# Squared-ReLU MLPs: relu without the norm factor on ScalarE, the factor squared at the addition to the residual

## The chip, the core and the metric

The kernel runs on one core of one Trainium2 chip. The metric is the device time of one execution in microseconds (us). Times of a kernel are given as the median of several runs. The engines are TensorE (PE, with its weight loads PEld), VectorE (DVE), ScalarE (ACT), GpSimd (POOL) and SyncE (SP, which only issues transfers here). Each works through its own queue in order; an instruction that has to wait holds up everything behind it on its engine.

## The reference

A two-layer model on 256 tokens of width 2048, all in float32: `h = h + attention(rms_norm(h))`, then `h = h + mlp(rms_norm(h))`, with stick-breaking attention in the first layer and native sparse attention in the second. Only the MLPs are touched here:

```
def rms_norm(x, g):
    xf = x.astype(jnp.float32)
    y = xf * lax.rsqrt(jnp.mean(xf * xf, axis=-1, keepdims=True) + NORM_EPS)
    return (y * g.astype(jnp.float32)).astype(x.dtype)

def sqrelu_mlp(h, w1, w2):
    return jnp.square(jax.nn.relu(h @ w1)) @ w2

# in reference(), for each of two layers, D_FF = 8192
h = h + sqrelu_mlp(rms_norm(h, mlp_norm_g[layer]), mlp_w1[layer], mlp_w2[layer])
```

The factor `rsqrt(...)` is one positive number r for each token. Since relu(r x) = r relu(x) for a positive r, and the square of it is r squared times relu(x) squared, r may enter before the relu or, squared, after the second product.

## The kernel before

**Products.** Every float32 product is made of three TensorE products of parts: a value is split into a rounded upper part `hi` and a rest `lo`, and hi*hi, hi*lo and lo*hi are summed in PSUM. The weights come from DRAM in blocks of 256 rows by 512 columns (512 KB) through SP's queue into a ring of five buffers `raw` and, in the MLPs, a sixth (`raw6`). ScalarE rounds a block to `hi` (L142), VectorE subtracts it to get `lo` (L144). A block is free for the next load when both have read it. `hi` and `lo` have four buffers each. Activations are kept split as well: `xs` holds the normed input of a layer without r (transposed, with the gains), `yhi` and `ylo` the activations behind the relu.

**MLP.** `mlp` treats d_ff in four quarters `fg`. Each quarter has two phases:

- `group1` makes the quarter's 2048 columns of `h @ w1` in four blocks `fb` of 512, transposed: the PSUM tiles have the d_ff index on the partitions and the tokens along the row. A block is 8 chunks (`chunk_T`, L206, 24 products of 256 columns). Behind it come the relu and the factor (L444), the square (L449, `sq`), the split into `yhi` (L450) and `ylo` (L451), and sums of it for the Strassen scheme (L456 to L460, `sums` to `ss`).
- `group2` multiplies with the quarter's rows of `w2`: blocks `nb` of 512 output columns, each of 8 chunks (`chunk_N`, L173, 12 products of 512 columns), added to the residual `h` by `add_h` (L383).

One or two of the four output blocks of a quarter are made by a one-level Strassen scheme instead (`in_S`, `chunk_S`, L269, 21 products of 256 columns with 7 sums in place of 8): block 2 in the shadow of `group2`, and block 3 in the shadow of the next quarter's `group1`. VectorE makes the sums of weights for it (`ts`, L245, L248, L249), ScalarE and VectorE split three quarters of the raw block into `shi` (L247) and `slo` (L250, one buffer each) and `ts` into `hi` and `lo`. Eight chunks make a block; then `add_S` adds the seven PSUM halves to `h` (L293 to L301). The very last block of the second MLP goes to `add_out`, which adds and writes the output.

**The factor.** `make_rstd` gives r with the tokens on the partitions. `group1` needs it along the row, so `rows` transposes it twice by `bcast_rows` (L376) and ScalarE copies it to `row` (L422), a tile of 256 float32 in each partition.

**Order.** The loops are unrolled. Outside the first stretch of the kernel a scheduler sets the order of each engine's queue from the order in which the code stands, the dependencies and its own costs. `spawn` and `pump` set small pieces of work between the products of a chunk.

Of the kernel before, what the change touches and what calls it, by code (L numbers as in the profile page):

```python
# [8 lines left out]
F32 = mybir.dt.float32  # L9
F32R = mybir.dt.float32r  # L10
AF = mybir.ActivationFunctionType
OP = mybir.AluOpType
# [3 lines left out]
P = 128  # L16
T = 256
NT = T // P
# [23 lines left out]
def hybrid_kernel(  # L42
# [6 lines left out]
    nc = tc.nc  # L49
# [11 lines left out]
    h = cpool.tile([P, NT, D], F32, name="h")  # L61
# [47 lines left out]
    def spawn(gen, rate, wait=0.0, first=False):  # L109
        beside.insert(0 if first else len(beside), [gen, rate, -wait])  # L110
# [54 lines left out]
    def bank(pool, tag):  # L165
        return pool.tile([P, NB], F32, tag=tag, name=tag)
# [117 lines left out]
        half = lambda j, i: bs[j][:, i * W:(i + 1) * W]  # L284
        return bs, [half(0, 0), half(1, 0), half(1, 1), half(2, 0), half(2, 1), half(3, 1), half(3, 0)]

    def add_S(nb, bs, ps, pool):

        W = NB // 2
        uv = pool.tile([P, 4, W], F32, tag="pre", name="uv", bufs=1)  # L290
        u, v = uv[:, :2, :], uv[:, 2:, :]
        hb = [h[:, t, nb * NB:(nb + 1) * NB] for t in range(NT)]
        nc.scalar.activation(u[:, 0, :], ps[0], AF.Copy)  # L293
        nc.vector.tensor_tensor(v[:, 0, :], ps[5], u[:, 0, :], op=OP.add)
        nc.vector.tensor_tensor(u[:, 1, :], ps[4], v[:, 0, :], op=OP.add)
        nc.vector.tensor_tensor(v[:, 1, :], ps[6], v[:, 0, :], op=OP.add)
        nc.vector.tensor_tensor(hb[0], bs[1], hb[0], op=OP.add)
        nc.vector.tensor_tensor(hb[1], bs[2], hb[1], op=OP.add)
        nc.vector.tensor_tensor(hb[0], hb[0], u.rearrange("p a n -> p (a n)"), op=OP.add)
        hv = hb[1].rearrange("p (a n) -> p a n", a=2)  # L300
        nc.vector.tensor_tensor(hv, hv, v[:, 1, :].unsqueeze(1).to_broadcast([P, 2, W]), op=OP.add)  # L301

    def proj_N(src, n0, pool=acc, tag="acc", turn=False):
        ps = [bank(pool, tag) for _ in range(NT)]
# [59 lines left out]
    def make_rstd(layer):  # L364
        s = small.tile([P, NT], F32, tag="ms", name="ms")
        nc.vector.tensor_reduce(s, ssq_t[layer], axis=AX.X, op=OP.add)
        nc.vector.tensor_scalar(s, s, 1.0 / D, EPS, op0=OP.mult, op1=OP.add)
        r = small.tile([P, NT], F32, tag="rstd", name="rstd")
        nc.gpsimd.tensor_tensor(r, s, neghalf[:, :NT], op=OP.pow)
        return r  # L370

    def bcast_rows(rstd):

        ps = bank(att, "att")
        for t in range(NT):
            nc.tensor.transpose(ps[:, t * P:(t + 1) * P], rstd[:, t:t + 1].to_broadcast([P, P]), ident)  # L376
        return ps

    def add_h(nb, ps, scale=None):
        for t in range(NT):  # L380
            hb = h[:, t, nb * NB:(nb + 1) * NB]
            if scale is None:
                nc.vector.tensor_tensor(hb, ps[t], hb, op=OP.add)  # L383
            else:
                nc.vector.scalar_tensor_tensor(hb, ps[t], scale[:, t:t + 1], hb, op0=OP.mult, op1=OP.add)

    def add_out(nb, ps, ov):

        for t in range(NT):
            for i in range(2):  # L390
                w = NB // 2
                c = slice(nb * NB + i * w, nb * NB + (i + 1) * w)
                nc.vector.tensor_tensor(h[:, t, c], ps[t][:, i * w:(i + 1) * w], h[:, t, c], op=OP.add)
                (nc.sync, nc.scalar)[i].dma_start(ov[:, t, c], h[:, t, c])

    def out_proj(src, layer, g0):
# [17 lines left out]
    def mlp(l, layer, junk, done, last=None):  # L414
        w1, w2 = mlp_w1[l], mlp_w2[l]
        ss = far(junk, KD * 4 * P, "ss").rearrange("p (a k i n) -> p a k i n", a=2, k=KD // 2, i=4)
        row = junk.tile([P, T], F32, name="row", bufs=1)

        def rows():
            yield  # L420
            pb = bcast_rows(make_rstd(layer))
            nc.scalar.activation(row, pb[:, :T], AF.Copy)  # L422

        def in_S(fg, nb):

            for i in range(NK):
                if i == 0:
                    bs, s = banks_S(att, "att")
                chunk_S(s, w2, fg * KD + i * KC, nb * NB, i == 0, i == NK - 1, yhi, ylo, ss[:, 0], ss[:, 1],
                        koff=fg * KD)  # L430
                if i == NK - 1:
                    add_S(nb, bs, s, junk)
                yield

        def group1(fg, beside_w1):

            step = lambda: next(beside_w1)
            for fb in range(D // NB):
                ps = [bank(acc, "acc") for _ in range(NB // P // 2)]
                proj_T(ps, w1, fg * D + fb * NB, then={2: step, 5: step} if beside_w1 else {})  # L440
                k, n = fb * (NB // P), NB // P
                a = junk.tile([P, n, T], F32, tag="pre", name="pre", bufs=1)
                for j in range(0, n, 2):
                    nc.vector.scalar_tensor_tensor(  # L444
                        a[:, j:j + 2, :], ps[j // 2].rearrange("p (m t) -> p m t", m=2), 0.0,
                        row.unsqueeze(1).to_broadcast([P, 2, T]), op0=OP.max, op1=OP.mult,
                    )
                s = junk.tile([P, n, T], F32, tag="sq", name="sq", bufs=1)
                nc.scalar.activation(s, a, AF.Square)  # L449
                nc.scalar.activation(yhi[:, k:k + n, :], s, AF.Copy)  # L450
                nc.vector.tensor_tensor(ylo[:, k:k + n, :], s, yhi[:, k:k + n, :].bitcast(F32), op=OP.subtract)  # L451

                sv = s.rearrange("p (j kk) t -> p j kk t", kk=2)
                a1, a2 = [[sv[:, :, kk, t * P:(t + 1) * P] for kk in (1, 0)] for t in range(NT)]
                q = junk.tile([P, 2, 4, P], F32, tag="sums", name="sums", bufs=1)
                nc.vector.scalar_tensor_tensor(q[:, :, 0, :], a2[0], -1.0, a2[1], op0=OP.mult, op1=OP.subtract)  # L456
                nc.vector.tensor_tensor(q[:, :, 2, :], a1[0], a2[0], op=OP.subtract)
                nc.vector.tensor_tensor(q[:, :, 1, :], a2[1], q[:, :, 2, :], op=OP.subtract)
                nc.vector.tensor_tensor(q[:, :, 3, :], a1[1], q[:, :, 1, :], op=OP.subtract)
                split_evac(ss[:, 0, k // 2:k // 2 + 2], ss[:, 1, k // 2:k // 2 + 2], q)  # L460

        def group2(fg, end):

            blocks = (0, 1, 3) if end else (0, 1)
            side, si = in_S(fg, 2), 0
            for j in range(len(blocks) * NK):
                nb, i = blocks[j // NK], j % NK
                if i == 0:
                    ps = [bank(acc, "acc") for _ in range(NT)]
                out = last is not None and end and nb == 3  # L470
                aside = si < NK and j >= 4 + (1.75 if end else 1.4) * si
                chunk_N(ps, w2, fg * KD + i * KC, nb * NB, i == 0, i == NK - (2 if out else 1), yhi, ylo,
                        koff=fg * KD, by_token=out and i == NK - 1,
                        turn=aside or (not end and j == len(blocks) * NK - 1))
                if i == NK - 1:
                    if out:
                        add_out(nb, ps, last)
                        return
                    add_h(nb, ps)
                    if end and nb == 3:  # L480
                        done(nb, (att, "att"))
                if aside:
                    next(side)
                    si += 1
                    if si == NK and end:
                        for n in range(3):
                            done(n, (att, "att"))

        spawn(rows(), 1)
        NK = KD // KC  # L490
        for fg in range(DFF // D):
            group1(fg, in_S(fg - 1, 3) if fg else None)
            group2(fg, fg == DFF // D - 1)


    with tc.tile_pool(name="sbp", bufs=2) as sp:
# [11 lines left out]
        with tc.manual_schedule(engines={mybir.EngineType.PE, mybir.EngineType.DVE, mybir.EngineType.Activation,  # L508
# [47 lines left out]
            for i in range(NX):  # L556
# [4 lines left out]
                first, last = i == 0, i + 1 == NX  # L561
# [11 lines left out]
        rows = sp.tile([P, 2, T], F32, name="rows", bufs=1)  # L573
        factor = []
# [90 lines left out]
        for hg in range(NH // HG):  # L665
            qT = sp.tile([P, HG, T], F32, name="qT")
            kT = far(sp, HG * T, "kT", F32, 2).rearrange("p (j t) -> p j t", j=HG)
            v = far(sp, NT * NB, "v", F32, 2).rearrange("p (t n) -> p t n", t=NT)
# [36 lines left out]
    with tc.tile_pool(name="nsa", bufs=2) as ap, ExitStack() as last:  # L705
# [283 lines left out]
        for i in range(2):  # L989
            cT = cp.tile([P, G, T], F32, tag="cT", name="cT", bufs=1)  # L990
            for b in range(2):
                ps = proj_Th(w_in, C0 + i * NB + b * T)
                if rstd is None:
                    rstd = make_rstd("nsa")
                    pb = bcast_rows(rstd)
# [58 lines left out]
        for g in range(G):  # L1054
            ps = [bank(acc, "acc") for _ in range(NT)]
# [9 lines left out]
            v = ap.tile([P, 2, NT, 2, P], F32R, tag="v", name="v")  # L1065
# [6 lines left out]
            ps = proj_N(w_in, g * NB)  # L1072
# [11 lines left out]
    with tc.tile_pool(name="m1p", bufs=2) as mp:  # L1084
        wsum = sixth = mp
        ov = out[0].rearrange("(t p) d -> p t d", p=P)
# [35 lines left out]
```

## Time and profile before

| | |
|---|---|
| median of 3 runs | 2154.17 us (2151.66 to 2154.63) |
| profiled execution, its own time | 2150.99 us |
| its span, first to last instruction | 2149.3 us |
| TensorE busy | 2138.9 us |
| VectorE busy | 1594.8 us |
| ScalarE busy | 1189.7 us |
| granted TensorE clock | 1.000 |
| first MLP, about | 392 to 1075 us of the span |
| second MLP, about | 1460 us to the end |

How to read the lines that follow. A group's line has the line of code, engine, operation, `output<-inputs`, the shapes, and then "busy us, mean ns of one | idle time of the engine before them, and what ended it". A line of time has start, duration, engine, line and operation, with the idle time before it in brackets. A stretch's line has the stretch, its length, the busy time of PE, PEld, DVE, ACT and POOL with the number of instructions, the granted TensorE clock, the busy share of the DMA engines and the rate in GB/s. Matmuls overlap, so how long one takes in a stream is read from start to start.

### The profile page before, as it was taken

Reading aid. Unit: us, or ns where it says so; the run is one execution under the profiler, and the core shown is the slowest. Engines: PE = TensorE matmul, PEld = TensorE weight load, DVE = VectorE, ACT = ScalarE, POOL = GpSimd, SP = SyncE. Lnnn points to the kernel's source line nnn. Section 1 sums busy time; section 2 is a strip of 40 time slices with the busy share of each in tenths; the row PEclk is TensorE's granted clock in tenths of the full one; section 3 lists DMA queues with packets and bytes.
Section 4 is the critical chain, followed back from the end, with each engine's and each line's share of the span. In section 5 each row is a group of like instructions: output and inputs, shape, how many; then the busy total and the mean of one; then the engine's idle time right before and its main releaser. Section 6 shows DMA issues by size and latency. Waiting matters only on the chain.

```text
span 2149.3 us, 37266 instructions
## 1 busy us (share of the span) xinstructions
PE 2138.9 (100%) x14898; PEld 1974.0 (92%) x14898; DVE 1594.8 (74%) x2193; ACT 1189.7 (55%) x1591; POOL 43.3 (2%) x75
## 2 busy tenths in 40 slices
PE   9999999999999999999999999999999999999999
PEld 9999988998998999999898888889989989989998
DVE  5556556668879878779776887755788798787796
ACT  6555665555555555455655666655555555554463
POOL 0000000000000000000000011000000000000000
PEclk9999999999999999999999999999999999999999
DMA  7655556665665656665667554456656556566654
GB/s 238 211 170 177 159 183 187 185 199 180 203 201 189 210 188 203 216 195 188 200 187 220 162 147 139 146 177 187 191 184 210 191 189 209 184 199 211 197 194 159
DMA packets 260790, 406.35 MB, mean 189 GB/s; under 512 B 13188, under 2 KB 91912, under 8 KB 260616
## 3 DMA queue, kind: packets, MB, share of 16 engines
q1 hardware_dynamic: 259800, 403.52, 59.9%
q8 instruction: 116, 1.90, 0.3%
q10 hardware_dynamic: 816, 0.46, 0.1%
q14 instruction: 58, 0.48, 0.1%
HBM read 401.83 MB, written 2.10 MB: 188 GB/s over the span
## 4 chain that ended last, share of the span: by engine, by line
PE 95%; DVE 3%; DMA 1%; issue 1%; ACT 0%; POOL 0%; DVEq 0%; SPq 0%; ACTq 0%; POOLq 0%
PE acc L206 42%; PE acc L173 35%; PE att L269 12%; PE att L173 1%; DVE lo L144 1%; DMA raw<-in_mlp_w_dram 1%; PE att L327 1%; PE att L944 1%; DVE slo L250 0%; DMA raw<-in_nsa_w_in_dram 0%; PE att L655 0%; PE att L607 0%; PE att L882 0%; PE att L938 0%; PE att L884 0%
## 5 line engine op out<-in xcount | busy, mean ns | idle before, releaser
L142 ACT ACTIVATE hi<-raw 128x1024 fp32r<-128x1024 f32 x639 | 673.1, 1058 | 511.3 <-PE acc L206 231.9
L144 DVE TENSOR_TENSOR lo<-raw,hi 128x1024 fp32r<-128x1024 f32 x639 | 774.1, 1221 | 214.6 <-ACT hi L142 199.7
L206 PE MATMUL acc<-xs,hi 128*128 128x256 f32 x5360 | 665.4, 277 | 0.0
L206 PEld LDWEIGHTS acc<-xs,hi 128*128 128x128 f32 x5360 | 634.6, 188 | 0.9
L206 PE MATMUL acc<-xs,lo 128*128 128x256 f32 x2680 | 359.2, 276 | 0.0
L206 PEld LDWEIGHTS acc<-xs,lo 128*128 128x128 f32 x2680 | 329.2, 188 | 0.0
L173 PE MATMUL acc<-hi,yhi 128*128 128x512 f32 x828 | 324.4, 392 | 0.0
L173 PE MATMUL acc<-hi,ylo 128*128 128x512 f32 x828 | 323.0, 390 | 0.0
L173 PE MATMUL acc<-lo,yhi 128*128 128x512 f32 x828 | 224.1, 391 | 0.0
L245 DVE TENSOR_TENSOR ts<-raw 128x512 f32<-128x512 f32 x112 | 76.8, 690 | 184.2 <-DMA raw<-in_mlp_w_dram 184.0
L142 ACT ACTIVATE hi<-ts 128x1024 fp32r<-128x1024 f32 x112 | 118.6, 1059 | 125.0 <-PE acc L173 47.3
L173 PEld LDWEIGHTS acc<-lo,yhi 128*128 128x128 f32 x828 | 154.6, 188 | 31.6
L173 PEld LDWEIGHTS acc<-hi,ylo 128*128 128x128 f32 x828 | 155.5, 188 | 29.6 <-DVE ylo L314 0.2
L173 PEld LDWEIGHTS acc<-hi,yhi 128*128 128x128 f32 x828 | 155.5, 188 | 29.6 <-ACT yhi L313 0.2
L173 PE MATMUL acc<-hi,xs 128*128 128x512 f32 x704 | 177.2, 392 | 0.0
L173 PEld LDWEIGHTS acc<-hi,xs 128*128 128x128 f32 x704 | 130.2, 188 | 26.2
L144 DVE TENSOR_TENSOR lo<-ts,hi 128x1024 fp32r<-128x1024 f32 x112 | 136.5, 1219 | 2.2 <-ACT hi L142 2.1
L247 ACT ACTIVATE shi<-raw 128x768 fp32r<-128x768 f32 x112 | 94.4, 843 | 77.6 <-DMA raw<-in_mlp_w_dram 28.3
L250 DVE TENSOR_TENSOR slo<-raw,shi 128x768 fp32r<-128x768 f32 x112 | 106.7, 952 | 2.6 <-PE att L269 2.5
L449 ACT ACTIVATE sq<-pre 128x1024 f32<-128x1024 f32 x32 | 34.0, 1063 | 128.5 <-DVE pre L444 128.5
L173 PE MATMUL acc<-lo,xs 128*128 128x512 f32 x352 | 97.0, 396 | 0.0
L269 PE MATMUL att<-hi,ss 128*128 128x256 f32 x672 | 94.4, 276 | 0.0
(249 smaller groups left out, 2170.6 us busy)
## 6 DMA issues: line engine op xcount, KB each, us to landing
raw<-in_mlp_w_dram SPq DMA_DIRECT2D x512, 512.0 KB, 4.4
raw<-in_sb_w_qkv_dram SPq DMA_DIRECT2D x95, 512.0 KB, 3.8
raw<-in_nsa_w_in_dram SPq DMA_DIRECT2D x50, 512.0 KB, 3.8
raw<-in_sb_w_out_dram SPq DMA_DIRECT2D x32, 512.0 KB, 3.9
raw<-in_nsa_w_in_dram SPq DMA_DIRECT2D x64, 256.0 KB, 3.9
raw<-in_nsa_w_out_dram SPq DMA_DIRECT2D x32, 512.0 KB, 3.6
w1t<-in_nsa_cmp_w_dram SPq DMA_DIRECT2D x8, 512.0 KB, 4.1
h<-in_x_dram SPq DMA_DIRECT2D x8, 256.0 KB, 4.5
```

Source lines behind the costliest of these rows:

```text
L142: nc.scalar.activation(hi, raw, AF.Copy)
L144: nc.vector.tensor_tensor(lo, raw, hi.bitcast(F32), op=OP.subtract)
L173: mm = lambda a, b, k, t, s, e: nc.tensor.matmul(ps[t], a[:, k, t * P:(t + 1) * P], b, start=s, stop=e)
L206: nc.tensor.matmul(o, w, x[:, k0 + kk, :], start=s, stop=e, skip_group_check=True)
L245: nc.vector.tensor_tensor(ts[:, :2, :], flat[:, W:3 * W].rearrange("p (a n) -> p a n", a=2), b12, op=OP.subtract)
L247: nc.scalar.activation(hi, flat[:, :3 * W], AF.Copy)
L250: nc.vector.tensor_tensor(lo, flat[:, :3 * W], hi.bitcast(F32), op=OP.subtract)
L269: nc.tensor.matmul(ps[i], a, w, start=s, stop=e, skip_group_check=True)
L327: nc.tensor.transpose(ps[:, j * T + t * P:j * T + (t + 1) * P], h[:, t, (kp + j) * P:(kp + j + 1) * P], ident)
L449: nc.scalar.activation(s, a, AF.Square)
L944: nc.tensor.transpose(ptp[:w, j * P:(j + 1) * P], src(j), ident)
```

## The change

The relu leaves VectorE: ScalarE makes it from PSUM, without the factor. `row`, its two transposes and its copy go. A tile `factor` of two numbers for each partition takes r squared (tokens on the partitions), and every addition of the MLP's output to `h` multiplies by it: `add_h` (a form that it has already), `add_S` and `add_out`. In `add_S` each of the four additions to `h` becomes a multiply-add.

```
-    def add_S(nb, bs, ps, pool):
+    def add_S(nb, bs, ps, pool, scale):
...
-        nc.vector.tensor_tensor(hb[0], bs[1], hb[0], op=OP.add)
-        nc.vector.tensor_tensor(hb[1], bs[2], hb[1], op=OP.add)
-        nc.vector.tensor_tensor(hb[0], hb[0], u.rearrange("p a n -> p (a n)"), op=OP.add)
-        hv = hb[1].rearrange("p (a n) -> p a n", a=2)
-        nc.vector.tensor_tensor(hv, hv, v[:, 1, :].unsqueeze(1).to_broadcast([P, 2, W]), op=OP.add)
+        f0, f1 = scale[:, 0:1], scale[:, 1:2]
+        add = lambda o, x, f: nc.vector.scalar_tensor_tensor(o, x, f, o, op0=OP.mult, op1=OP.add)
+        add(hb[0], bs[1], f0)
+        add(hb[1], bs[2], f1)
+        add(hb[0], u.rearrange("p a n -> p (a n)"), f0)
+        add(hb[1].rearrange("p (a n) -> p a n", a=2), v[:, 1, :].unsqueeze(1).to_broadcast([P, 2, W]), f1)
...
-                nc.vector.tensor_tensor(h[:, t, c], ps[t][:, i * w:(i + 1) * w], h[:, t, c], op=OP.add)
+                nc.vector.scalar_tensor_tensor(
+                    h[:, t, c], ps[t][:, i * w:(i + 1) * w], scale[:, t:t + 1], h[:, t, c], op0=OP.mult, op1=OP.add
+                )
...
-        row = junk.tile([P, T], F32, name="row", bufs=1)
-
-        def rows():
+        factor = junk.tile([P, NT], F32, name="factor", bufs=1)
+
+        def factors():
             yield
-            pb = bcast_rows(make_rstd(layer))
-            nc.scalar.activation(row, pb[:, :T], AF.Copy)
+            r = make_rstd(layer)
+            nc.vector.tensor_tensor(factor, r, r, op=OP.mult)
...
-                    add_S(nb, bs, s, junk)
+                    add_S(nb, bs, s, junk, factor)
...
-                    nc.vector.scalar_tensor_tensor(
-                        a[:, j:j + 2, :], ps[j // 2].rearrange("p (m t) -> p m t", m=2), 0.0,
-                        row.unsqueeze(1).to_broadcast([P, 2, T]), op0=OP.max, op1=OP.mult,
-                    )
+                    nc.scalar.activation(a[:, j:j + 2, :], ps[j // 2].rearrange("p (m t) -> p m t", m=2), AF.Relu)
...
-                        add_out(nb, ps, last)
+                        add_out(nb, ps, last, factor)
...
-                    add_h(nb, ps)
+                    add_h(nb, ps, factor)
```

In the changed kernel's lines `pre` is written at L447, `add_h` stands at L386 and the additions of `add_S` at L298; other lines above 300 move by one to three.

More of the change, by code (lines that the diff above doesn't have):

```diff
@@ L385, in add_h, with add_out @@
                 nc.vector.scalar_tensor_tensor(hb, ps[t], scale[:, t:t + 1], hb, op0=OP.mult, op1=OP.add)
-    def add_out(nb, ps, ov):
+    def add_out(nb, ps, ov, scale):
         for t in range(NT):
@@ L487, in group2 @@
                             done(n, (att, "att"))
-        spawn(rows(), 1)
+        spawn(factors(), 1)
         NK = KD // KC
```

## The prediction

> **What bounds the kernel now.** I read the busy table first, then the chain that ended last, then who waited for whom on TensorE, and at last the MLPs stretch by stretch. A share below is of the span of 2149.3 us.
>
> ```profile
> PE 2138.9 (100%) x14898; PEld 1974.0 (92%) x14898; DVE 1594.8 (74%) x2193; ACT 1189.7 (55%) x1591; POOL 43.3 (2%) x75
> ...
> PE 95%; DVE 3%; DMA 1%; issue 1%; ACT 0%; POOL 0%; DVEq 0%; SPq 0%; ACTq 0%; POOLq 0%
> ```
>
> TensorE is busy from end to end and makes up 95% of the chain; VectorE has 3% of it, ScalarE nothing. So work that moves from VectorE to ScalarE counts only where a matmul waits for it. The waits of TensorE and its weight loads, from the table of waits (the columns are total us, times, longest us):
>
> ```profile
> PE att L269 <- DVE slo L250: 3.5, 5, 1.1
> ...
> PEld att L269 <- DVE slo L250: 5.1, 7, 1.3
> ```
>
> Only one kind of wait touches the MLPs: the products of a Strassen chunk (L269) wait for its lower half `slo`. How much that costs shows when the second phases of the d_ff quarters are laid side by side: each runs 16 ordinary chunks and 8 Strassen chunks in the same order. In the table by stretch the columns are the stretch, its length, then busy time of PE, PEld, DVE, ACT, POOL. The last row is a first phase (32 ordinary chunks and 8 Strassen chunks).
>
> ```profile
> 480.18:543.09 62.91, 62.91 (x363) 55.19 (x362) 53.25 (x69) 35.41 (x37) 0.00 (x0) 1.00 0.61 202
> 649.18:712.50 63.32, 63.18 (x363) 55.25 (x362) 57.37 (x78) 34.62 (x37) 0.00 (x0) 1.00 0.60 199
> 818.60:881.92 63.32, 63.32 (x362) 55.38 (x362) 56.65 (x76) 34.59 (x37) 0.00 (x0) 1.00 0.61 194
> 1548.24:1612.24 64.00, 63.50 (x363) 55.37 (x362) 50.94 (x67) 34.70 (x37) 0.00 (x0) 1.00 0.60 191
> 1718.17:1784.14 65.97, 64.00 (x364) 55.65 (x363) 56.91 (x76) 34.83 (x38) 0.00 (x0) 1.00 0.56 186
> 1890.23:1954.57 64.34, 63.21 (x363) 55.28 (x362) 58.59 (x79) 35.29 (x38) 0.00 (x0) 1.00 0.60 197
> ...
> 543.10:649.20 106.10, 106.10 (x937) 106.10 (x937) 81.72 (x101) 56.26 (x59) 0.00 (x0) 1.00 0.61 195
> ```
>
> The first stretch is undisturbed (62.91). The others exceed it by 0.41, 0.41, 1.09, 3.06 and 1.43, together 6.4 us. That is nearly all a faster VectorE could win back in the MLPs.
>
> **The change part by part.** The sum is made against the profiled execution (2150.99 us; span 2149.3). The median of the runs, 2154.17, lies 3.2 us above it, so I add the same sum to that.
>
> ```profile
> L444 DVE SCALAR_TENSOR_TENSOR pre<-acc,row 128x512 f32<-128x512 f32 x64 | 41.1, 683 | 7.5 <-PE acc L206 7.4
> L313 ACT ACTIVATE pT<-att 128x512 fp32r<-128x512 f32 x24 | 14.1, 586 | 5.9 <-PE att L944 5.8
> L383 DVE TENSOR_TENSOR h<-acc,h 128x512 f32<-128x512 f32 x50 | 32.2, 684 | 9.2 <-PE acc L173 9.2
> L317 DVE SCALAR_TENSOR_TENSOR q<-att,gq,q 128x512 fp32r<-128x512 f32 x8 | 5.9, 733 | 0.0
> L422 ACT ACTIVATE row<-att x2: 385/385/385, 406.8 to 1474.8; 128x256 f32<-128x256 f32 x2
> ...
> L376 PE MATMUL att<-ident,rstd 128*128 128x128 f32 x8 | 1.5, 271 | 0.0
> ```
>
> *Relu.* VectorE loses 64 operations of 683 ns (41.1 us). ScalarE gains 64 of about 586 ns, by the copy of the same shape out of PSUM (37.5 us), and loses the two copies of `row` (385 ns each). In a first phase ScalarE goes from 56.3 of 106.1 us to about 61; it stays idle for over 40%. The order at the end of the second quarter's first phase in the second MLP, ScalarE before:
>
> ```order
> 911 L142 ACTIVATE hi<-raw_18503 128x1024
> 912 L142 ACTIVATE hi<-raw 128x1024
> 913 L449 ACTIVATE sq<-pre 128x1024
> 914 L142 ACTIVATE hi<-raw 128x1024
> 915 L450 ACTIVATE yhi<-sq 128x1024
> ```
>
> and the changed kernel there:
>
> ```order
> 931 L142 ACTIVATE hi<-raw_18497 128x1024
> 932 L142 ACTIVATE hi<-raw 128x1024
> 933 L447 ACTIVATE pre<-acc 128x512 x2
> 934 L449 ACTIVATE sq<-pre 128x1024
> 935 L142 ACTIVATE hi<-raw 128x1024
> ```
>
> The relus stand where the square stood, which already waited there:
>
> ```profile
> 1717.16 1.99 ACT L142 ACTIVATE hi<-raw 128x1024 fp32r<-128x1024 f32 x2
> 1723.99 1.06 ACT L449 ACTIVATE sq<-pre 128x1024 f32<-128x1024 f32 x1 [4.84 <-DVE pre L444]
> ```
>
> Two relus take 1.2 us from 1719.15, so the square ends near 1721.4 instead of 1725.05, and the `hi` behind it comes 3.6 us sooner. ScalarE pays nothing on the path: 0. The Trainium skill says the opposite of this step: "ScalarE: Activation LUTs", section "Rules for kernel authors", puts relu on VectorE, up to about 3 times faster in bf16. The rows have ScalarE shorter for this f32 shape out of PSUM (586 against 683 ns). With the page's factor two relus would take 4.1 us and the square would still start no later than it does now, so the sum is the same by both; only the slow rival gets 1 in 100 from it.
>
> *Transposes.* Four of the eight `bcast_rows` transposes go (two for each MLP): half of 1.5 us, so -0.75 us on TensorE itself. The product of the factor with itself (128x2) and its later need, at the first add to `h` instead of the first relu, are off every queue that waits.
>
> *Additions to h.* 34 in `add_h` (50 less the 16 of the two output projections) and 56 in `add_S` (4 in each of 14) read a scalar per token: 733 ns instead of 684, so 90 x 49 ns = 4.4 us more on VectorE, which gains 36.7 us net. The very last one, in `add_out`, is on the path: +0.05 us.
>
> *What the 36.7 us release.* The longest backlog of VectorE runs from 1717 into the stretch with the largest loss. In time order, VectorE there:
>
> ```profile
> 1739.43 1.22 DVE L144 TENSOR_TENSOR lo<-raw,hi 128x1024 fp32r<-128x1024 f32 x1
> ...
> 1743.10 1.22 DVE L144 TENSOR_TENSOR lo<-raw,hi 128x1024 fp32r<-128x1024 f32 x1
> 1744.95 0.69 DVE L245 TENSOR_TENSOR ts<-raw 128x512 f32<-128x512 f32 x1 [0.64 <-DMA raw<-in_mlp_w_dram]
> 1745.68 0.42 DVE L248 TENSOR_TENSOR ts<-ts,raw 128x256 f32<-128x256 f32 x1
> 1746.02 0.95 DVE L250 TENSOR_TENSOR slo<-raw,shi 128x768 fp32r<-128x768 f32 x1
> ...
> 1740.68 4.25 DMA raw<-in_mlp_w_dram
> ...
> 1747.03 0.50 PE L269 MATMUL att<-slo,yhi 128*128 128x256 f32 x2 [0.47 <-DVE slo L250]
> ```
>
> `slo` stands behind the `ts` of a chunk two further on, and that waits for a transfer which SP could issue only when the `lo` of 1739.43 had freed a buffer. Without the two `pre` (1.2 us from start to start) and with four dearer additions (0.2 us) that `lo` ends 1.0 us sooner, and the transfer lands near 1743.9. But the order moves too. VectorE before, from the `ts` of 1740.57 to `slo`:
>
> ```order
> 1461 L245 TENSOR_TENSOR ts<-raw 128x512
> 1462 L144 TENSOR_TENSOR lo<-ts,hi 128x1024
> 1463 L248 TENSOR_TENSOR ts<-ts,raw 128x256
> 1464 L249 TENSOR_TENSOR ts<-raw,ts 128x256
> 1465 L144 TENSOR_TENSOR lo<-raw,hi 128x1024
> 1466 L245 TENSOR_TENSOR ts<-raw 128x512
> 1467 L248 TENSOR_TENSOR ts<-ts,raw 128x256
> 1468 L250 TENSOR_TENSOR slo<-raw,shi 128x768
> ```
>
> and changed:
>
> ```order
> 1425 L245 TENSOR_TENSOR ts<-raw 128x512
> 1426 L248 TENSOR_TENSOR ts<-ts,raw 128x256
> 1427 L249 TENSOR_TENSOR ts<-raw,ts 128x256
> 1428 L144 TENSOR_TENSOR lo<-ts,hi 128x1024
> 1429 L245 TENSOR_TENSOR ts<-raw 128x512
> 1430 L144 TENSOR_TENSOR lo<-raw,hi 128x1024
> 1431 L248 TENSOR_TENSOR ts<-ts,raw 128x256
> 1432 L250 TENSOR_TENSOR slo<-raw,shi 128x768
> ```
>
> A `lo` now stands behind the waiting `ts` instead of ahead of it, between it and `slo`: landing 1743.95, then 0.6, 1.14 and 0.33 us of start-to-start time put `slo` at 1746.05, against 1746.02. The 1.0 us gained is spent there. Bounds for all such waits: -6.4 us (all vanish) and +4.9 us (that `lo`, 1.22 us, late in the four quarters with this order, and nothing gained). I take 0, by this place.
>
> *Addresses.* `row` took 1024 bytes of each partition, `factor` takes 32. By the built programs everything after it in that pool moves down 992 bytes: the sixth load buffer, `pre`, `sq`, `sums`, `ts`, `shi`, `slo`. 992 is 15.5 times 64, so `shi` and `slo`, which began at a multiple of 64, now begin 32 past one. TensorE streams both as moving operands: x224 each in the rows `shi,yhi`, `shi,ylo`, `shi,ss` and `slo,yhi`, x112 in `slo,ss`, 1008 in all, first and last here with two time rows of other products:
>
> ```profile
> L269 PE MATMUL att<-shi,yhi x224: 276/277/283, 493.6 to 2126.7; 128*128 128x256 f32 x112
> ...
> L269 PE MATMUL att<-slo,ss x112: 276/276/286, 495.5 to 2128.3; 128*128 128x256 f32 x112
> ...
> 1702.19 1.98 PE L206 MATMUL acc<-xs,hi 128*128 128x256 f32 x16
> 1704.01 1.07 PE L206 MATMUL acc<-xs,lo 128*128 128x256 f32 x8
> ...
> 1201.32 0.28 PE L882 MATMUL att<-khi,q 128*128 128x264 f32 x1
> ...
> 1202.04 1.09 PE L173 MATMUL acc<-lo,xs 128*128 128x512 f32 x4
> ```
>
> Sixteen products of 256 columns take 1.82 us from start to start, 113.8 ns each; six of 264 columns, back to back, 0.72 us, 120 ns each. Eight more columns cost 6.2 ns where their share is 3.6. That looks like a stream in pieces of 16 columns (64 bytes) at 7.1 ns, where a half piece at the end costs a whole one. No row shows 256 columns that begin half a piece late; they touch 17 pieces instead of 16. Bounds: 0 and 7.1 ns a product, 0 and 7.2 us in all. The 264-column row, the nearest, shows one of two half pieces billed in full: 3.55 ns, x 1008 = +3.6 us. It falls on TensorE, which nothing covers.
>
> The Trainium skill, "TensorE: Matmul & The Clock Gate", section "Back-to-back issue gap", makes the gap depend on the column count alone, N/2.4 + 2.5 ns. That is 109.2 and 112.5 ns, 3.3 apart; the trace has 113.8 and 120, 6.2 apart, so they differ just where it matters. By the page this term would be 0; that is the first rival.
>
> Sum: -0.75 + 0.05 + 0 + 3.6 = +2.9 us: 2153.9 for the profiled execution, **2157** for the median.
>
> **The rivals.** *Addresses cost nothing:* the sum is -0.7, the time 2153.5. For it: a multiple of 64 bytes need not be what TensorE reads in. Against it: the 264-column row. *A whole piece for each product* (the slower side): 1008 x 7.1 = 7.2 us, time 2160.6. It is slower beyond 0.2% once a product costs more than (4.3 + 0.7) / 1008 = 5.0 ns. For it: 264 columns are billed 17 pieces of 7.1 (120.7) almost in full; against it: there the piece ends the stream, here it is split between the two ends. *VectorE's relief reaches TensorE* and addresses cost nothing: 4 to 6.4 us of waits vanish, time 2147 to 2149.5. For it: VectorE was busy without a gap up to 1744.3; against it: the place worked out above, and that these waits end in a transfer, which a freer VectorE doesn't shorten.
>
> **How the numbers follow.** Forecast 0.40 (2155 to 2159.5), addresses free 0.33 (2151 to 2156), whole pieces 0.20 (2159 to 2163), relief 0.07. A difference below 0.2%, 4.3 us, is about what a measurement of this kernel cannot tell from none. Faster beyond that (under 2149.9) is the relief and a tail of the second case: 0.07. Slower (over 2158.5) is the whole-piece case and the upper eighth of the forecast: 0.25. The rest, 0.68, is the same. The range 2150.5 to 2161.5 leaves out the relief and the ends of the bounds.
>
> **What would show it.** Relus of 580 to 600 ns on ScalarE and none on VectorE; additions to `h` near 733 ns; the undisturbed stretch of 62.91 us with its eight Strassen chunks at 63.17 (72 products x 3.55 ns) if the forecast's price holds, 62.9 if addresses are free, 63.4 for whole pieces; the six stretches' excess still near 6 us. I am wrong if the first stretch stays at 62.9, or if the sum of excesses moves by more than 3 us.

## The result and the profile after

The changed kernel takes 2173.97 us (median of 5 runs, 2172.32 to 2175.78) against 2154.63 (5 runs, 2151.66 to 2157.65): ratio 1.0096, interval 1.0085 to 1.0108. That is 19.3 us more, where 2.9 were predicted, and beyond the range. The profiled execution takes 2172.32 us, 21.3 more than the one of before.

The busy table and the shares of the chain, as shown of before:

```profile
PE 2163.3 (100%) x14894; PEld 2000.6 (92%) x14894; DVE 1569.7 (72%) x2131; ACT 1235.9 (57%) x1653; POOL 45.2 (2%) x75
...
PE 98%; DVE 1%; DMA 0%; ACT 0%; issue 0%; POOL 0%; SPq 0%; DVEq 0%; ACTq 0%; POOLq 0%
```

TensorE holds more of the chain than before (98% against 95) and VectorE less: nothing new makes it wait. It does four instructions fewer and is busy 24 us longer. So the products themselves have become slower, and the granted clock is 1.000 in both profiles. The new operations are what they were taken for:

```profile
L447 ACT ACTIVATE pre<-acc 128x512 f32<-128x512 f32 x64 | 34.2, 586 | 0.5 <-DVE h L298 0.5
L386 DVE SCALAR_TENSOR_TENSOR h<-acc,factor,h 128x512 f32<-128x512 f32 x34 | 23.9, 743 | 3.1 <-PE acc L173 3.1
L298 DVE SCALAR_TENSOR_TENSOR h<-att,factor,h 128x512 f32<-128x512 f32 x28 | 20.8, 744 | 2.9 <-PE att L269 2.9
```

All that TensorE waits for now, in the table of waits (us, times, longest):

```profile
PE att L515 <- POOL ident masks.py:199: 1.6, 1, 1.6
PE acc L534 <- ACT hi L527: 0.8, 1, 0.8
PE att L789 <- DVE hs L784: 0.5, 1, 0.5
PE att L836 <- DVE kc L831: 0.4, 1, 0.4
```

The waits for `slo` are gone. Stretch by stretch, the six second phases that the prediction laid side by side, and a first phase:

```profile
479.32:542.81 63.49, 63.49 (x362) 55.88 (x361) 50.19 (x64) 35.97 (x39) 0.00 (x0) 1.00 0.58 192
652.79:716.27 63.48, 63.48 (x362) 55.88 (x361) 54.28 (x70) 36.26 (x39) 0.00 (x0) 1.00 0.61 197
826.25:889.73 63.48, 63.48 (x362) 55.88 (x361) 53.97 (x71) 36.28 (x39) 0.00 (x0) 1.00 0.61 195
1560.47:1624.28 63.81, 63.81 (x362) 55.99 (x361) 50.05 (x64) 35.85 (x39) 0.00 (x0) 1.00 0.59 188
1734.26:1797.74 63.48, 63.48 (x362) 55.88 (x361) 54.49 (x70) 36.24 (x39) 0.00 (x0) 1.00 0.60 197
1907.72:1971.20 63.48, 63.48 (x362) 55.88 (x361) 53.94 (x70) 36.26 (x39) 0.00 (x0) 1.00 0.60 195
...
542.81:652.79 109.98, 109.98 (x937) 109.98 (x936) 83.92 (x104) 60.93 (x65) 0.00 (x0) 1.00 0.62 198
```

Two things are to be seen. The second phases are even now: their undisturbed length rose from 62.91 to 63.48, and the excess over it fell from 6.4 us in all to 0.33, in one stretch. And the first phase with Strassen chunks in it, which by the prediction's price (72 products x 3.55 ns) would have come to about 106.4, went from 106.1 to 110.0. There are six of those, and all six take 109.98 now. The balance: 6 x 3.88 = 23.3, 8 second phases x 0.57 = 4.6, waits -6.1, transposes -0.75 (the prediction's estimate), together about +21 of the 21.3 measured.

Where in the first phase? The chain of waits of both kernels in the same place (start, length, engine, tile, line, products; L206 are ordinary products, L269 a Strassen chunk), before:

```profile
543.09 8.17 PE acc L206 x72
551.26 2.38 PE att L269 x21
553.64 8.16 PE acc L206 x72
561.80 2.38 PE att L269 x21
564.18 13.60 PE acc L206 x120
```

and after:

```profile
542.97 8.17 PE acc L206 x72
551.14 2.48 PE att L269 x21
553.62 8.48 PE acc L206 x72
562.10 2.48 PE att L269 x21
564.58 14.13 PE acc L206 x120
```

Up to the first Strassen chunk the 72 ordinary products take 8.17 us in both, 113.4 ns each. Behind it they take 8.48, 117.8 ns each, and so on to the end of the phase. Yet `xs`, which they stream, and their weights `hi` and `lo` stand where they stood. Only the chunk between them has operands that moved. 864 of a phase's 936 products stand at or behind that chunk (696 of L206, 168 of L269), and 864 x 4.4 ns = 3.8 us is the whole loss of the phase.

### The profile page after: what moved, and what is told of

It is laid out like the page before. It is cut to its first block, busy times and chain, and to the rows that moved or that the text cites. A ratio compares the mean times of both kernels' runs of the same rounds, so it can differ in the third digit from the quotient of the medians.

```text
span 2170.6 us, 37272 instructions
## 1 busy us (share of the span) xinstructions
PE 2163.3 (100%) x14894; PEld 2000.6 (92%) x14894; DVE 1569.7 (72%) x2131; ACT 1235.9 (57%) x1653; POOL 45.2 (2%) x75
## 4 chain that ended last, share of the span: by engine, by line
PE 98%; DVE 1%; DMA 0%; ACT 0%; issue 0%; POOL 0%; SPq 0%; DVEq 0%; ACTq 0%; POOLq 0%
PE acc L206 43%; PE acc L173 36%; PE att L269 13%; PE att L173 1%; PE att L944 1%; PE att L328 1%; DMA raw<-in_nsa_w_in_dram 0%; DVE lo L144 0%; PE att L655 0%; PE att L607 0%; PE att L882 0%; PE att L938 0%; PE att L884 0%; PE att L883 0%; PE att L936 0%; PE att L937 0%
## 5 line engine op out<-in xcount | busy, mean ns | idle before, releaser
L206 PE MATMUL acc<-xs,hi 128*128 128x256 f32 x5360 | 677.5, 279 | 0.0
L206 PEld LDWEIGHTS acc<-xs,hi 128*128 128x128 f32 x5360 | 646.0, 188 | 1.0
L206 PE MATMUL acc<-xs,lo 128*128 128x256 f32 x2680 | 365.4, 279 | 0.0
L206 PEld LDWEIGHTS acc<-xs,lo 128*128 128x128 f32 x2680 | 335.1, 189 | 0.0
L269 PE MATMUL att<-hi,ss 128*128 128x256 f32 x672 | 97.3, 281 | 0.0
L269 PEld LDWEIGHTS att<-hi,ss 128*128 128x128 f32 x672 | 86.6, 188 | 0.0
```

The source lines that it names most:

```text
L206: nc.tensor.matmul(o, w, x[:, k0 + kk, :], start=s, stop=e, skip_group_check=True)
L269: nc.tensor.matmul(ps[i], a, w, start=s, stop=e, skip_group_check=True)
```

## The experiments

These theories had to be told apart: the start addresses of `shi` and `slo` slow TensorE and the slow pace outlasts the products that read them (A, with a state); each product pays for its own operand only (A'); the relu on ScalarE or the new order slows TensorE (B); and, of the address itself, which offsets count (C, D, E). The ratios below are to the kernel before on the same chip. A Strassen chunk has 21 products; where an expectation counts 23, it is 21.

**Addresses undone.**

```
-        factor = junk.tile([P, NT], F32, name="factor", bufs=1)
+        factor = junk.tile([P, T], F32, name="factor", bufs=1)[:, :NT]
```

> The changed kernel with `factor` in a tile of 1024 bytes of each partition, so that every tile of that pool stands where it stood before; nothing else differs. Theory A (the start addresses of shi and slo slow TensorE, and the 256-column products that follow them too): L206 back from 116.2 to 114.0 ns a product, the waits for slo still gone, so 2154.6 - 0.7 (transposes) - 6 (waits) = about 2148 us. Rival B (relu on ScalarE out of PSUM, or the new order on VectorE and ScalarE, slows TensorE): addresses change nothing, about 2174 us as the changed kernel.

Measured: 2144.88 us against 2152.63 of the kernel before, ratio 0.9967 (0.9955 to 0.9979). Both lengths of before are back, first and second phase, and no product of the MLPs waits for `slo`:

```profile
542.69:648.78 106.09, 106.09 (x938) 106.09 (x936) 82.05 (x102) 60.29 (x65) 0.00 (x0) 1.00 0.62 203
648.78:711.69 62.91, 62.91 (x363) 55.18 (x362) 55.11 (x72) 36.29 (x39) 0.00 (x0) 1.00 0.60 201
```

B falls: every instruction of the change is in this kernel. It is also faster than both kernels, by 0.33% than the one before.

**Addresses alone.**

```
-        row = junk.tile([P, T], F32, name="row", bufs=1)
+        row = junk.tile([P, T + 8], F32, name="row", bufs=1)[:, :T]
```

> The kernel before with 32 bytes more in the tile `row`, so that the sixth load buffer, pre, sq, sums, ts, shi and slo start 32 bytes later; no instruction differs. Theory A: 19.3 us of the change and the 6.7 us that the change won elsewhere come to +26 us at most, so 2174 to 2181 us, with L206 at 116.2 ns a product. Rival B: 2154.6 us, no change.

Measured: 2172.55 us, ratio 1.0097 (1.0082 to 1.0111), with the instructions of the kernel before:

```profile
543.45:653.43 109.98, 109.98 (x937) 109.97 (x936) 84.59 (x107) 57.01 (x59) 0.00 (x0) 1.00 0.59 191
653.43:716.91 63.48, 63.48 (x362) 55.88 (x361) 56.01 (x74) 35.04 (x37) 0.00 (x0) 1.00 0.60 199
```

The two lengths are those of the changed kernel to 0.01 us. The time is below the 2174 to 2181 expected, since the waits for `slo` are gone here too, without any relief of VectorE: a slower TensorE gives VectorE more time, it seems. So their absence in the changed kernel doesn't by itself show what the lighter VectorE is worth; that took the runs with the addresses kept.

**`shi` alone, `slo` alone**, the rest of the pool where it stood:

```
-        hi, lo = [wsum.tile([P, 3 * W], F32R, tag=n, name=n, bufs=1) for n in ("shi", "slo")]
+        hi = wsum.tile([P, 3 * W + 32], F32R, tag="shi", name="shi", bufs=1)[:, 8:8 + 3 * W]
+        lo = wsum.tile([P, 3 * W], F32R, tag="slo", name="slo", bufs=1)
```

(for `slo` alone, the same two changes are on the other line).

> As the first of these runs (all tiles where they stood before), but only shi starts 32 bytes past a multiple of 128; slo and all else at a multiple of 128. Theory A with a state that one such product sets and that stays until 512-column products come: nearly the whole loss, 2170 to 2174 us. Rival A' (each product pays for its own operand, and what follows is slowed by something else): only the 672 products of shi pay, 672 x 4.5 ns = 3 us, about 2151 us.

> As the first of these runs, but only slo starts 32 bytes past a multiple of 128. Theory A with a state: in the first phases the products of slo set it and the loss is again nearly whole; in the second phases only the last 7 of 23 products of a chunk run slow, so some 2 to 3 us less, 2167 to 2172 us. Rival A': 336 x 4.5 ns = 1.5 us, about 2150 us.

Measured: 2173.52 us (ratio 1.0101, 1.0087 to 1.0116) with `shi`, 2168.37 (1.0080, 1.0062 to 1.0097) with `slo`. The phases with `shi` displaced:

```profile
542.91:652.89 109.98, 109.98 (x938) 109.97 (x936) 83.00 (x103) 60.80 (x65) 0.00 (x0) 1.00 0.62 197
652.89:716.55 63.66, 63.66 (x362) 55.91 (x361) 54.59 (x71) 36.24 (x39) 0.00 (x0) 1.00 0.59 198
```

and with `slo`:

```profile
542.78:652.67 109.89, 109.89 (x938) 109.89 (x936) 83.80 (x104) 60.62 (x65) 0.00 (x0) 1.00 0.62 201
652.67:715.71 63.04, 63.04 (x362) 55.40 (x361) 54.19 (x70) 36.24 (x39) 0.00 (x0) 1.00 0.59 194
```

Either one brings the loss of a first phase almost whole, the three products a chunk that read `slo` (109.89) about as much as the six that read `shi` (109.98). Nothing that is paid for each displaced product can do that; A' falls. In the second phases, where 512-column products follow each chunk, `slo`, which is read late in the chunk, costs only 0.13 us. (In the run with `shi`, `slo` lies 128 bytes off modulo 256, which costs something by itself, as seen below.)

**One displaced chunk of 112.** `shi` and `slo` start 32 bytes later in the ninth chunk only, the first of a first phase:

```
+        chunks += 1
+        o = 8 if chunks == 9 else 0
...
+        hi, lo = [wsum.tile([P, 3 * W + 32], F32R, tag=n, name=n, bufs=1)[:, o:o + 3 * W] for n in ("shi", "slo")]
```

> All tiles where they stood before, and of the 112 Strassen chunks only one, the first in the first phase of the second d_ff quarter of the first MLP, takes its shi and slo 32 bytes later. State theory: its 9 products set the state, and it holds through the 7 aligned chunks and all ordinary products behind it up to the phase's end: that phase 110.0 instead of 106.1 us, the other five first phases 106.1, in all 2144.9 + 3.9 = 2148.8 us. Rival (each chunk sets and pays for itself): 23 products x 4.4 ns = 0.1 us, up to 0.5 us if the products up to the next chunk pay too.

Measured: 2147.26 us, ratio 0.9986 (0.9977 to 0.9994). The time alone lies between the two forecasts and nearer the state theory's. The phases tell it otherwise (the displaced one first, then another first phase, then a second phase):

```profile
543.98:650.31 106.33, 106.33 (x937) 106.33 (x936) 81.14 (x101) 60.17 (x65) 0.00 (x0) 1.00 0.62 203
713.38:819.63 106.25, 106.25 (x937) 106.25 (x936) 81.13 (x100) 60.28 (x65) 0.00 (x0) 1.00 0.62 200
650.31:713.38 63.07, 63.07 (x362) 55.34 (x361) 55.55 (x73) 36.04 (x39) 0.00 (x0) 1.00 0.60 200
```

No state held: the displaced chunk itself takes 2.48 us where the others of its phase take 2.40, and the 72 ordinary products behind it take 8.16 again. Instead every phase is 0.16 us longer (14 x 0.16 = 2.2 us, nearly all of the 2.4 by which the run exceeds the one with addresses undone). The tile for the spare 32 floats had moved `slo` by 128 bytes in all chunks (and so by 160 in the displaced one), and the run changed two things. Its repetition gives `shi` a tile of `3 * W + 128` floats, so that all starts are the old ones modulo 512, and those of the changed kernel in the one chunk:

> As the run with one displaced chunk, but now both shi and slo keep their starts of before modulo 512 in 111 chunks, and exactly those of the changed kernel in the one (there slo stood 128 bytes off in all chunks, and the state ended with that chunk's own last products). State theory: the first phase of the second d_ff quarter at 110.0 us, the other five at 106.1, 2144.9 + 3.9 = 2148.8 us. Rival (the next aligned chunk ends the state): 0.4 to 0.6 us more in that phase, about 2145.4 us.

Measured: 2149.35 us, ratio 0.9983 (0.9971 to 0.9995); 3.1 us above the 256-byte kernel on the same chip (below), where 3.9 were expected. The displaced phase and the next first phase:

```profile
544.77:654.70 109.93, 109.93 (x937) 109.93 (x936) 82.62 (x103) 60.22 (x65) 0.00 (x0) 1.00 0.62 197
717.60:823.69 106.09, 106.09 (x938) 106.09 (x936) 82.46 (x102) 60.72 (x65) 0.00 (x0) 1.00 0.63 200
```

And TensorE in time order, from the end of the displaced chunk into the next one, whose operands are all aligned:

```profile
555.42 2.05 PE L206 MATMUL acc<-xs,hi 128*128 128x256 f32 x16
...
563.90 0.28 PE L275 MATMUL att<-shi,yhi 128*128 128x256 f32 x1
...
566.37 0.40 PE L206 MATMUL acc<-xs,hi 128*128 128x256 f32 x2
```

From 555.42 to 563.90 stand 72 ordinary products, 117.8 ns each; the aligned chunk from 563.90 to 566.37 takes 117.6 ns a product, where an aligned chunk took 113.3 before. Nine products that begin 32 bytes late slow some 850 that follow, none of which reads a displaced operand, until the phase ends. That is the state, shown.

**Ending it.** The changed kernel, its misaligned `shi` and `slo` kept, with the last four products of each chunk moved:

```
-        thi, tlo = split(ts)
+        thi, tlo = split(ts, (0, FAR))
```

> The changed kernel with its misaligned shi and slo, but the `lo` of a Strassen chunk's sums, which the chunk's last four products stream, 64 bytes later, so that the chunk ends in products whose operand agrees with the weights in its start mod 128, as the ordinary products of 512 columns do. If such products end the slow state: the ordinary products after a chunk at 113.4 ns, the loss down to the chunks' own products, about 2155 us. If it takes 512 columns, or the coming back to aligned operands sets the state anew: 2172 to 2176 us.

Measured: 2158.11 us, ratio 1.0029 (1.0015 to 1.0044). A first and a second phase and, behind a chunk, the ordinary products:

```profile
714.45:821.50 107.05, 107.05 (x938) 107.05 (x936) 82.29 (x101) 60.54 (x65) 0.00 (x0) 1.00 0.63 200
821.50:885.26 63.76, 63.76 (x362) 55.96 (x361) 54.55 (x71) 36.29 (x39) 0.00 (x0) 1.00 0.60 193
```

```profile
555.63 1.07 PE L206 MATMUL acc<-xs,lo 128*128 128x256 f32 x8
556.54 1.18 PE L206 MATMUL acc<-xs,hi 128*128 128x256 f32 x9
```

Eight products in 0.91 us, 113.8 ns: fast again, though the chunk before them was slow. The first phase loses 1.0 us instead of 3.9. The second phase gains nothing, it even loses a little more than in the changed kernel (63.76 against 63.48). In all, 64 bytes more on a third operand take 16 us off the 2173.97 of the changed kernel; products of 256 columns are enough to end the state.

**Which offsets count.** The changed kernel with `factor` in 64, 128 and 256 bytes (`[P, 16]`, `[P, 32]`, `[P, 64]`, of which `[:, :NT]` is used), and the kernel with addresses undone with only `shi` and `slo` moved: both get tiles of `3 * W + 32` floats and start 16 bytes later in them (`[:, 4:4 + 3 * W]`). As in the first run with one displaced chunk, the longer tile moves `slo` by another 128 bytes:

> The changed kernel with `factor` in 64 bytes instead of 32: shi, slo and the rest of the pool now start 64 past a multiple of 128. Theory C (what counts is a start off a multiple of 64 bytes): no loss, about 2145 us as with all addresses of before. Theory D (what counts is the distance from the weights' start, 64 past a multiple of 128, which is now 0 instead of 64): the products of shi and slo at 118 to 120 ns, and if the state holds, about 2170 us as with 32 bytes.

> All tiles where they stood before, shi and slo 16 bytes past a multiple of 128. Theory C: any start off a multiple of 64 sets the slow state, about 2172 us. Theory E (32 bytes are the unit; a shift below it costs nothing): 2145 us.

> The changed kernel with `factor` in 128 bytes, so that shi, slo and the rest of the pool start 128 bytes off where they stood before modulo 256, but the same modulo 128. If 128 is the period: about 2145 us, first phases at 106.1. If 256 is the period: products of shi and slo near 117 ns; 2147 to 2150 us where the state does not hold (first phases near 106.6), 2170 us where it does.

> The changed kernel with `factor` in 256 bytes: shi, slo and the rest of the pool as before modulo 256, not modulo 512. If 256 (or less) is the period: 2144.9 us, first phases at 106.1 and undisturbed second phases at 62.9. If 512 is the period: 2147 to 2172 us.

| start of shi and slo, past that of before modulo 256 | time, us | ratio to before | first phase | second phase |
|---|---|---|---|---|
| 16, `slo` 144 | 2172.70 | 1.0101 (1.0082 to 1.0119) | 109.99 | 63.32 |
| 32 (the change) | 2173.97 | 1.0096 (1.0085 to 1.0108) | 109.98 | 63.48 |
| 64 | 2151.10 | 0.9999 (0.9989 to 1.0008) | 106.58 | 63.33 |
| 128 | 2151.39 | 0.9994 (0.9982 to 1.0007) | 106.51 | 63.45 |
| 256, that is 0 | 2146.26 | 0.9968 (0.9955 to 0.9980) | 106.09 | 62.91 |

The phases of 16, 64, 128 and 256 bytes, in this order:

```profile
544.76:654.75 109.99, 109.99 (x938) 109.99 (x936) 83.91 (x104) 60.77 (x65) 0.00 (x0) 1.00 0.62 200
654.75:718.07 63.32, 63.32 (x363) 55.72 (x361) 54.41 (x70) 36.24 (x39) 0.00 (x0) 1.00 0.60 196
```

```profile
543.12:649.70 106.58, 106.58 (x938) 106.57 (x937) 82.58 (x103) 60.59 (x65) 0.00 (x0) 1.00 0.63 203
649.70:713.03 63.33, 63.33 (x362) 55.60 (x361) 55.08 (x72) 36.27 (x39) 0.00 (x0) 1.00 0.60 201
```

```profile
545.00:651.51 106.51, 106.51 (x937) 106.51 (x936) 82.00 (x102) 60.40 (x65) 0.00 (x0) 1.00 0.63 202
651.51:714.96 63.45, 63.45 (x363) 55.72 (x362) 55.33 (x72) 36.28 (x39) 0.00 (x0) 1.00 0.61 203
```

```profile
542.62:648.71 106.09, 106.09 (x937) 106.08 (x936) 79.33 (x98) 59.55 (x65) 0.00 (x0) 1.00 0.62 202
...
1718.37:1781.28 62.91, 62.91 (x362) 55.19 (x361) 54.49 (x72) 36.30 (x39) 0.00 (x0) 1.00 0.59 198
```

E falls (16 bytes cost as much as 32). C and D each hold in part. Displacements of 16 or 32 bytes left the lasting state behind them; but that every start off a multiple of 64 does so is not shown, for the chunk with `shi` 32 and `slo` 160 bytes off left none. At 64 and 128 bytes a phase loses 0.4 to 0.5 us, which is paid within the chunks (2.43 to 2.46 us in place of 2.38) and doesn't last: the 72 ordinary products behind a chunk take 8.16 us. Both have the transposes and waits saved, so against the 2144.9 us of the run with addresses undone they lose some 6 us and come out level with the kernel before. Of these five only whole 256 bytes cost nothing: both lengths are back. In that profile TensorE still waited for `slo` twice, 1.3 us in all, and one second phase took 63.93 us; the two runs with one displaced chunk show 1.1 and 2.3 us of such waits. So the waits don't vanish from every execution.

**The relu alone,** with the addresses of before:

```
-                    nc.vector.scalar_tensor_tensor(a[:, j:j + 2, :], ..., 0.0, row..., op0=OP.max, op1=OP.mult)
+                    nc.scalar.activation(a[:, j:j + 2, :], ps[j // 2].rearrange("p (m t) -> p m t", m=2), AF.Relu)
```

> The kernel before, all addresses kept, with only the relu moved to ScalarE; it leaves out the multiplication by the norm factor (row is still built, and nothing reads it). If the relief of VectorE alone removes the waits for slo: 2145 to 2147 us, no such wait in the table of waits. If the waits went by the new order or by the later need of the factor: 2150 to 2155 us with waits for slo as before.

Measured: 2147.06 us, ratio 0.9971 (0.9958 to 0.9984), about 6 us less than before, and TensorE waits for `slo` nowhere. So moving the relu is worth nearly the whole gain by itself, with additions and transposes as they were. The run doesn't separate VectorE's smaller load from the new order of its queue, which came with it, nor from the relu no longer needing the factor.

## Why the prediction was wrong

*Relu, transposes, additions: right.* The relu takes 586 ns on ScalarE as forecast, and TensorE never waits for it. The additions take 743 to 744 ns instead of 733, off the path as said. Of the eight transposes (1.5 us of TensorE) four are left (0.8 us); their gain is too small to be seen in the time.

*Addresses: the right term, sized eight times too small; this is the step that failed.* The prediction found the 992 bytes and the start 32 past a multiple of 64, and priced them at 3.55 ns for each of the 1008 products that stream `shi` and `slo`. The addresses cost 23.3 + 4.6 = 27.9 us. The price for one product was near (4.4 ns); the count was wrong, since it is paid by nearly every 256-column product behind the first displaced one, whatever it reads: 6 x 864 in the first phases and 8 x 168 in the second ones, some 6500. That the price was near is luck: the reading in pieces of 64 bytes behind it charges only products whose own operand begins within a piece, and nothing for a shift of 64 bytes, which cost 0.06 us a chunk. The bounds of 0 and 7.2 us took both ends from the same count, so neither could hold the case. All three forecasts for the first second-phase stretch, 62.9, 63.17 and 63.4, were missed by the 63.49 measured (that of whole pieces by little), and the first phase, where most of the loss lies, had no forecast of its own. Of the rivals, "addresses cost nothing" falls, and with it a spacing by column count alone: the same 72 products of 256 columns took 8.17 us ahead of a chunk and 8.48 behind it. The Trainium skill ("TensorE: Matmul & The Clock Gate", section "Back-to-back issue gap") gives N/2.4 + 2.5 ns for an isolated product, says that in a stream the weight loads set the spacing too, and has no term for the start of an operand in either. These rows show one.

*What the 36.7 us release: taken as 0, measured about -6.* The run with addresses undone and the one with the relu alone both lose the waits, as the last rival said, and the excess of the six stretches moved by 6.1 us, twice what the prediction named as a sign of being wrong. The reading of the place near 1745 kept the start of VectorE's backlog where it stood and took only the two `pre` out of it. VectorE before, and then in the kernel with addresses undone (the second phase starts at 1718.17 and 1716.12):

```profile
1716.40 0.69 DVE L245 TENSOR_TENSOR ts<-raw 128x512 f32<-128x512 f32 x1 [4.03 <-DMA raw<-in_mlp_w_dram]
```

```profile
1711.65 0.69 DVE L245 TENSOR_TENSOR ts<-raw 128x512 f32<-128x512 f32 x1 [1.74 <-DMA raw<-in_mlp_w_dram]
...
1739.68 0.69 DVE L245 TENSOR_TENSOR ts<-raw 128x512 f32<-128x512 f32 x1 [1.80 <-DMA raw<-in_mlp_w_dram]
...
1741.76 0.95 DVE L250 TENSOR_TENSOR slo<-raw,shi 128x768 fp32r<-128x768 f32 x1
```

The backlog begins with a `ts` that waits for a transfer. It started 1.8 us ahead of the phase's start before and starts 4.5 ahead now. The later `ts` follows its transfer at 23.6 us into the phase instead of 26.8, and `slo` at 25.6 instead of 27.9. The order did move a `lo` in front of `slo`, as the prediction showed, and its price was paid; but VectorE had freed buffers sooner, and a freed buffer lets a transfer start sooner. The chain before shows it for the first of these `ts`: its transfer was issued at 1711.27, right behind a `lo` that ended at 1711.25, and took 5.12 us. Over the whole span SP's queue waited 1332.7 us for `lo` before and 1263.3 with addresses undone. So against the prediction's argument that a freer VectorE doesn't shorten a transfer: it starts it earlier. Of the 6.1 us that vanished in the changed kernel itself, how much is due to this and how much to the slower TensorE can't be told apart: either alone took the waits away in a profile (the relu alone, and the addresses alone).

## What to carry to other kernels

A tile that shrinks moves everything behind it in its pool; give it its old size, or one that keeps the starts of TensorE's operands the same modulo 256 bytes, before judging the change by its time. When products slow down whose own operands haven't moved, look from start to start for the product behind which the pace changes. A cost per instruction needs two questions, how much and how many pay, and the bounds of the sum have to cover both.

## What the runs showed of the hardware

- TensorE's pace for 256-column products has at least two steady values at the same granted clock of 1.000, 113.4 and 117.8 ns, and a product can leave the slow one behind for hundreds of others: nine that began 32 bytes late cost 3.8 us in the 850 that followed.
- It ended with products that stand otherwise: the 512-column products of the second phase (the next first phase begins with 72 products in 8.17 us), or four 256-column products 64 bytes further on (8 products in 0.91 us behind them).
- The products behind a chunk were slow (72 in 8.48 us) with `shi` and `slo` 32 and 32, 0 and 32, 32 and 128, or 16 and 144 bytes off, and fast (8.16) with 64 and 64, 128 and 128, or 32 and 160. What rule lies behind this list stays open.
- In the kernel's code the weights of the 256-column products lie 64 bytes (`FAR`) into their tiles and the moving operands at the start of theirs. What inside TensorE keeps the pace, and whether the start by itself or its distance from the weights' sets it, these runs leave open; no run moved the weights.
